# Up projection of an encoder block: first operands and weight sums issued ahead of the last token tile's norm, partial results kept in the u tile

## The chip, the cores and the metric

One program on one core of a Trainium2 chip. The metric is the device time of one execution in microseconds (us); the time of the kernel before is the median of three runs. Engines are TensorE (PE in the profile, PEld for its weight loads), VectorE (DVE), ScalarE (ACT), GpSimd (POOL) and SyncE (SP), which here issues the DMAs.

## The reference, cut to what matters

One layer of an encoder block on 1024 tokens of width 1024: a token mixer, a cross-attention into 256 memory tokens, and a gated MLP. Each has an RMSNorm before and after. What the change touches is the passage from the cross-attention's output to the MLP:

```python
y = memory_cross_attention(h, mem_n, w_mem_q[l], w_mem_kv[l], w_mem_o[l])
x = x + rmsnorm(y, norm_mem_post[l])
h = rmsnorm(x, norm_ffn_pre[l])
y = conv_gated_ffn(h, w_up[l], ffn_dw[l], ffn_dw_b[l], w_down[l])
...
def conv_gated_ffn(h, w_up, ffn_dw, ffn_dw_b, w_down):
    u = jnp.einsum("bsd,df->bsf", h, w_up)                # 1024 -> 2 x 2816
    u = dwconv_centred(u, ffn_dw, ffn_dw_b)               # width 3, along the tokens
    gate, val = u[..., :D_FF], u[..., D_FF:]
    return jnp.einsum("bsf,fd->bsd", jax.nn.gelu(gate, approximate=True) * val, w_down)
```

## The kernel before, in words

**Number format.** Every f32 operand of a matmul is split into a high part (a ScalarE cast) and a low part (source minus high part, on VectorE or GpSimd). A product is then three matmuls: high by high, high by low, low by high (`gemm3_multi`, lines 94 to 101).

**Cross-attention output (lines 701 to 712).** For each of eight token tiles (128 tokens), `cross_gemm` multiplies by the eight weight tiles `Uw`. `cross_norm` does the rest: a square with a sum on ScalarE (line 609), the reciprocal root on GpSimd (lines 85 and 86), scaling and residual on VectorE (lines 611 and 612), a store of x2, then a second square (709), a second root and the scaling to `h3` (711).

**Operands of the up projection's token side (lines 714 to 736).** `cross_operands` transposes h3 on TensorE, copies it to the raw tiles `b11`, `b21` (tokens 0 to 511) or `b12`, `b22` (the others), and from token tile 4 on forms the differences t1 to t4 (line 697), each in the place of a tile that it no longer needs. `b_split` (lines 688 to 694) makes high and low parts. Differences are on VectorE except t3, which is on GpSimd.

**Up projection (lines 752 to 827).** The product of the weights and tokens, each as 2 by 2 blocks, is done with seven block products in place of eight. There are 22 feature indices `fi`; each takes a gate tile `rg` and a value tile `rv` of the weights. `up_first(fi)` splits rg into `a1` and makes products p1 and p2, which need b11 and b21 alone, so tokens 0 to 511. `up_operands(fi)` forms the weight sums s12 and s34 on GpSimd from rg and rv (lines 775 to 778) and splits them into `a2`, `a3` and `a22`. `up_finish(fi)` does the other five products with t1, t2, b22, t3 and t4, adds up the quarters of `u`, runs the convolution, GELU and the product of gate and value, and stores the result. A half-finished sum stands in a tile `q`. After token tile 7's norm the kernel issues `up_first` for fi 0 and 1, then `cross_operands(7)`; from then on `up_first(fi)`, `up_operands(fi)`, `up_finish(fi - 1)`.

**What sets the order.** The program is written with a tile framework. It places each engine's instructions at compile time by a timeline of its own; the order on each engine is then fixed and the engine runs its queue in order. Tiles of one tag share a fixed number of buffers, and a later tile of a tag takes its buffer behind the earlier ones. Tag "w" has seven buffers (Uw, then a1, u, a2, a3, a22), tag "tmp" four (x2, h3, q, s12, s34), "raw" three (x1r, wg, wv), "a" fifteen (the operands' high and low parts among them), PSUM tag "B" four (pTs, p1 to p7).

Of the kernel before, what the change touches and what calls it, by code (L numbers as in the profile page):

```python
# [33 lines left out]
def encoder_block(ctx: ExitStack, tc: tile.TileContext, x, xT, mem, w_a, w_q, w_kv, w_mkv, w_mqT,  # L34
                  w_mo, w_out, w_up, w_down, cols, rows, g10, rope, out):
    nc = tc.nc
# [16 lines left out]
    def tmp(name):  # L53
        return tmpp.tile([128, 1024], F32, tag="tmp", name=name)
# [55 lines left out]
    def W(shape, name):  # L110
        return wp.tile([128] + shape, F32R, tag="w", name=name)
# [503 lines left out]
    def load_raw(src, name):  # L615
        r = raw(name)
        nc.sync.dma_start(out=r, in_=src)
        return r
# [21 lines left out]
    for t in range(8):  # L640
        h, tt = t // 4, t % 4
        y = psS("y1")
        tok_gemm(y, mxh[h], mxl[h], wo, tt)
        xr = gE[:, 1, :]
# [3 lines left out]
        j = tmp("junk2")  # L648
# [40 lines left out]
    def b_split(name, ts_):  # L689
        if name not in BO:  # L690
            BO[name] = (A([4, 512], f"{name}h"), A([4, 512], f"{name}l"))
        src, (hi, lo) = BR[name], BO[name]
        nc.scalar.copy(out=hi[:, :, ts_], in_=src[:, :, ts_])
        nc.vector.tensor_tensor(out=lo[:, :, ts_], in0=src[:, :, ts_], in1=f(hi[:, :, ts_]), op=ALU.subtract)

    def b_sub(dst, in0, in1, ts_, eng):
        eng.tensor_tensor(out=BR[dst][:, :, ts_], in0=BR[in0][:, :, ts_], in1=BR[in1][:, :, ts_], op=ALU.subtract)
# [14 lines left out]
        return j  # L712

    def cross_operands(t, j):
        h, tt = t // 4, t % 4
        ts_ = slice(tt * 128, tt * 128 + 128)
        if t == 4:
            BR["b12"], BR["b22"] = A([4, 512], "r_b12", F32), A([4, 512], "r_b22", F32)
            BR["t1"], BR["t2"], BR["t3"], BR["t4"] = BR["b11"], BR["b22"], BR["b12"], BR["b21"]
        for g in range(2):  # L720
            p = psB("pTs")
            for k in range(4):
                tr(p[:, k * 128:k * 128 + 128], j[:, (4 * g + k) * 128:(4 * g + k + 1) * 128])
            nc.scalar.copy(out=BR[f"b{g + 1}{h + 1}"][:, :, ts_], in_=p.rearrange("p (k t) -> p k t", k=4))
        if h == 0:
            b_split("b11", ts_)
            b_split("b21", ts_)
        else:
            b_sub("t1", "b12", "b11", ts_, nc.vector)
            b_split("t1", ts_)  # L730
            b_split("b22", ts_)
            b_sub("t3", "b22", "b12", ts_, nc.gpsimd)
            b_sub("t2", "b22", "t1", ts_, nc.vector)
            b_split("t2", ts_)
            b_split("t3", ts_)
            b_sub("t4", "t2", "b21", ts_, nc.vector)
            b_split("t4", ts_)
# [3 lines left out]
    def a_split(dst, src, eng):  # L741
        nc.scalar.copy(out=dst[:, 0, :], in_=src)  # L742
        eng.tensor_tensor(out=dst[:, 1, :], in0=src, in1=f(dst[:, 0, :]), op=ALU.subtract)  # L743
# [8 lines left out]
    H0, H1 = slice(0, 512), slice(512, 1024)  # L752
    ups, firsts, rgs = {}, {}, {}

    def up_first(fi):

        rg = rgs.pop(fi) if fi in rgs else load_raw(w_up[fi, 0], "wg")
        a1 = W([2, 2, 512], "a1")
        a_split(a1[:, 0], rg[:, H0], nc.gpsimd)
        a_split(a1[:, 1], rg[:, H1], nc.gpsimd)  # L760
        u = wp.tile([128, 2, 1024], F32, tag="w", name="u")
        q = tmp("q")
        p1, p2 = psB("p1"), psB("p2")
        product(p1, a1[:, 0], "b11")
        nc.scalar.copy(out=q[:, H0], in_=p1)
        product(p2, a1[:, 1], "b21")
        nc.vector.tensor_tensor(out=u[:, 0, H0], in0=p2, in1=q[:, H0], op=ALU.add)
        firsts[fi] = (rg, u, q)

    def up_operands(fi):  # L770

        rg, u, q = firsts.pop(fi)
        rv = load_raw(w_up[fi, 1], "wv")
        s12, s34 = tmp("s12"), tmp("s34")
        nc.gpsimd.tensor_tensor(out=s12[:, H0], in0=rv[:, H0], in1=rv[:, H1], op=ALU.add)
        nc.gpsimd.tensor_tensor(out=s12[:, H1], in0=s12[:, H0], in1=rg[:, H0], op=ALU.subtract)
        nc.gpsimd.tensor_tensor(out=s34[:, H0], in0=rg[:, H0], in1=rv[:, H0], op=ALU.subtract)
        nc.gpsimd.tensor_tensor(out=s34[:, H1], in0=rg[:, H1], in1=s12[:, H1], op=ALU.subtract)
        a2, a3 = W([2, 2, 512], "a2"), W([2, 2, 512], "a3")
        a_split(a2[:, 0], s12[:, H1], nc.vector)  # L780
        a_split(a2[:, 1], s12[:, H0], nc.vector)
        a_split(a3[:, 0], s34[:, H1], nc.vector)
        a_split(a3[:, 1], s34[:, H0], nc.vector)
        if fi % 2 == 0:
            a22[0] = W([2, 2, 512], "a22")
        a_split(a22[0][:, fi % 2], rv[:, H1], nc.gpsimd)
        ups[fi] = (a2, a3, a22[0][:, fi % 2], u, q)
# [41 lines left out]
    UP_PRE = 2  # L829
    for t in range(8):  # L830
        if t == 6:
            for fi in range(UP_PRE):
                rgs[fi] = load_raw(w_up[fi, 0], "wg")
        j = cross_norm(t, *cross_gemm(t))
        if t == 7:
            for fi in range(UP_PRE):
                up_first(fi)
        cross_operands(t, j)
# [248 lines left out]
```

## Time and profile before

| | |
|---|---|
| median of three runs | 1479.98 us (1477.62 to 1480.1) |
| profiled execution | 1478.46 us; span from first to last instruction 1476.7 us |
| busy share of the span | PE 94%, PEld 79%, DVE 74%, POOL 48%, ACT 47% |
| mean granted TensorE clock | 0.983 of full speed |

The span is 1.8 us less than the profiled execution's time. Busy shares are averages over stages with different limits: the token tiles' norms and operands of the passage between two matmul stages take 758 to 800 us of the span, the up projection runs on to about 1205 us, the down projection to the end.

### The profile page before, as it was taken

Reading aid. Unit: us, or ns where it says so; the run is one execution under the profiler, and the core shown is the slowest. Engines: PE = TensorE matmul, PEld = TensorE weight load, DVE = VectorE, ACT = ScalarE, POOL = GpSimd, SP = SyncE. Lnnn points to the kernel's source line nnn. Section 1 sums busy time; section 2 is a strip of 40 time slices with the busy share of each in tenths; the row PEclk is TensorE's granted clock in tenths of the full one; section 3 lists DMA queues with packets and bytes.
Section 4 is the critical chain, followed back from the end, with each engine's and each line's share of the span. In section 5 each row is a group of like instructions: output and inputs, shape, how many; then the busy total and the mean of one; then the engine's idle time right before and its main releaser. Section 6 shows DMA issues by size and latency. Waiting matters only on the chain.

```text
span 1476.7 us, 18881 instructions
## 1 busy us (share of the span) xinstructions
PE 1392.0 (94%) x7020; PEld 1165.0 (79%) x7020; DVE 1099.4 (74%) x1323; ACT 700.5 (47%) x1192; POOL 707.2 (48%) x627
## 2 busy tenths in 40 slices
PE   7999999889999999999997999999999997978895
PEld 5889988678988888888875888888888875756784
DVE  7499898899999534335468777777777789996676
ACT  6325653688888424334435444444444443323442
POOL 6628787711111414002137555444445449697456
PEclk9999999999999999999998999999999999999998
DMA  6316770000000524013223222222222292334145
GB/s 208 128 48 207 260 237 15 20 1 1 1 2 29 178 94 141 31 43 129 93 79 114 87 86 86 86 87 86 86 87 79 95 375 100 106 130 143 42 130 192
DMA packets 49515, 152.77 MB, mean 103 GB/s; under 512 B 9104, under 2 KB 9360, under 8 KB 49424
## 3 DMA queue, kind: packets, MB, share of 16 engines
q1 hardware_dynamic: 49424, 151.58, 30.8%
q8 instruction: 55, 0.90, 0.3%
q14 instruction: 36, 0.29, 0.1%
HBM read 119.05 MB, written 32.51 MB: 103 GB/s over the span
## 4 chain that ended last, share of the span: by engine, by line
PE 65%; DVE 15%; POOL 6%; issue 5%; DMA 5%; ACT 3%; SPq 0%; POOLq 0%; DVEq 0%; ACTq 0%
PE p L97 9%; PE p L98 9%; PE p L100 9%; DVE op L891 4%; PE y L98 4%; PE y L100 4%; PE y L97 4%; PE pPT L81 3%; PE sc L100 2%; PE sc L97 2%; PE sc L98 2%; DVE acts L891 2%; PE po L555 2%; PE sp L524 2%; PE sp L525 2%
## 5 line engine op out<-in xcount | busy, mean ns | idle before, releaser
L91 PE MATMUL yd<-op 128*128 128x512 f32 x308 | 126.8, 413 | 31.9 <-DVE op L891 16.0
L295 DVE SCALAR_TENSOR_TENSOR cacc<-conv,col,cacc 128x1009 f32<-128x1009 f32 (+14 forms) x120 | 145.8, 1273 | 4.7 <-ACT cacc L242 4.5
L92 PE MATMUL yd<-op 128*128 128x512 f32 x308 | 123.4, 404 | 1.8 <-DVE op L891 1.7
L923 ACT CAST op<-acts 128x512 fp32r<-128x512 f32 x77 | 47.6, 621 | 129.9 <-PE yd L92 47.6
L891 DVE TENSOR_TENSOR op<-acts,op 128x512 fp32r<-128x512 f32 x77 | 88.7, 1158 | 26.0 <-ACT op L923 25.8
L742 ACT CAST a<-s 128x512 fp32r<-128x512 f32 x88 | 50.6, 620 | 113.4 <-PE p L100 55.4
L91 PEld LDWEIGHTS yd<-op 128*128 128x128 f32 x308 | 60.2, 196 | 55.1 <-POOL op L891 23.5
L90 PE MATMUL yd<-op 128*128 128x512 f32 x308 | 98.4, 394 | 0.0
L743 POOL TENSOR_TENSOR a<-wg,a 128x512 fp32r<-128x512 f32 x44 | 62.5, 1441 | 72.9 <-ACT a L742 72.9
L793 DVE SCALAR_TENSOR_TENSOR c<-u,col,c 128x1023 f32<-128x1023 f32 x44 | 56.7, 1288 | 49.4 <-ACT c L792 49.3
L743 DVE TENSOR_TENSOR a<-s,a 128x512 fp32r<-128x512 f32 x88 | 72.3, 835 | 27.8 <-ACT a L742 27.5
L545 DVE TENSOR_TENSOR PL<-pPT,PH 128x512 fp32r<-128x512 f32 x128 | 82.7, 680 | 5.0 <-ACT PH L544 4.6
L85 POOL TENSOR_SCALAR rt<-ss 128x1 f32<-128x1 f32 (+1 forms) x43 | 13.0, 302 | 150.4 <-ACT x L609 75.8
L527 DVE TENSOR_REDUCE nm<-sp 128x1 f32<-128x1024 f32 x64 | 78.0, 1219 | 2.9 <-PE sp L525 1.8
L530 ACT ACTIVATE P<-sp,nm 128x1024 f32<-128x1024 f32 x64 | 72.2, 1128 | 8.9 <-PE pPT L81 5.1
L792 ACT ACTIVATE c<-u,col 128x1024 f32<-128x1024 f32 x44 | 53.2, 1210 | 48.7 <-DVE u L803 46.8
L544 ACT CAST PH<-pPT 128x512 fp32r<-128x512 f32 x128 | 69.3, 593 | 13.5 <-PE pPT L81 12.7
L92 PEld LDWEIGHTS yd<-op 128*128 128x128 f32 x308 | 60.1, 195 | 16.2 <-DVE op L891 4.2
L81 PE MATMUL pPT<-ident,P 128*128 128x128 f32 x512 | 68.6, 274 | 3.7 <-DVE PL L545 2.3
L90 PEld LDWEIGHTS yd<-op 128*128 128x128 f32 x308 | 58.8, 191 | 12.6
L81 PEld LDWEIGHTS pPT<-ident,P 128*128 128x128 f32 x512 | 58.6, 140 | 12.3 <-DVE PL L545 3.9
L743 POOL TENSOR_TENSOR a<-wv,a 128x512 fp32r<-128x512 f32 x22 | 31.9, 1468 | 74.6 <-ACT a L742 60.5
(352 smaller groups left out, 4553.7 us busy)
## 6 DMA issues: line engine op xcount, KB each, us to landing
st<-in_w_down_dram SPq DMA_DIRECT2D x43, 512.0 KB, 3.8
wg<-in_w_up_dram SPq DMA_DIRECT2D x22, 512.0 KB, 4.1
wv<-in_w_up_dram SPq DMA_DIRECT2D x22, 512.0 KB, 3.9
act_d<-u SPq DMA_DIRECT2D x22, 512.0 KB, 2.9
acts<-act_d SPq DMA_DIRECT2D x22, 512.0 KB, 9.1
wmkv_r<-in_w_mkv_dram SPq DMA_DIRECT2D x16, 512.0 KB, 4.0
x_d<-x SPq DMA_DIRECT2D x16, 512.0 KB, 2.9
wmq_r<-in_w_mqT_dram SPq DMA_DIRECT2D x8, 512.0 KB, 3.5
```

What stands on the lines that cost most here:

```text
L81: nc.tensor.transpose(out=out_, in_=in_, identity=ident)
L90: nc.tensor.matmul(out=ps, lhsT=sh, rhs=mh, start=first, stop=False)
L91: nc.tensor.matmul(out=ps, lhsT=sh, rhs=ml, start=False, stop=False)
L92: nc.tensor.matmul(out=ps, lhsT=sl, rhs=mh, start=False, stop=last)
L97: nc.tensor.matmul(out=p, lhsT=sh, rhs=mh, start=first, stop=False)
L98: nc.tensor.matmul(out=p, lhsT=sh, rhs=ml, start=False, stop=False)
L100: ins = nc.tensor.matmul(out=p, lhsT=sl, rhs=mh, start=False, stop=last)
L295: nc.vector.scalar_tensor_tensor(out=acc[:, t0:t1_], in0=a[:, t0 + o:t1_ + o], scalar=cc(C_DW + c * 31 + j), in1=acc[:, t0:t1_], op0=ALU.m ...
L527: nc.vector.reduce_max(out=nm, in_=sp, axis=AX.X, negate=True)
L545: nc.vector.tensor_tensor(out=PL[dst], in0=p3, in1=f(PH[dst]), op=ALU.subtract)
L743: eng.tensor_tensor(out=dst[:, 1, :], in0=src, in1=f(dst[:, 0, :]), op=ALU.subtract)
L891: eng.tensor_tensor(out=dst, in0=in0, in1=in1, op=op)
```

## The change

1. `up_first`'s split of the weights becomes `up_first_operands(fi, engs)`, where the two low parts can go to different engines. For fi 0 and 1 it is called after token tile 7's matmuls and before its norm, with one low part on GpSimd and one on VectorE; in the other iterations it stays where it was, with both on GpSimd.
2. The load of rv and the four weight sums become `up_sums(fi)`, called for fi 0 right after token tile 7's norm, before `up_first` of 0 and 1.
3. `q` is no longer a tile of tag "tmp" but the second half of `u`.
4. In `cross_operands` of tokens 512 and up, b22 is split before t1, and token tile 7's t3 is formed on VectorE.

```diff
     def cross_operands(t, j):
+        third = nc.gpsimd if t < 7 else nc.vector
...
             b_sub("t1", "b12", "b11", ts_, nc.vector)
+            b_split("b22", ts_)
             b_split("t1", ts_)
-            b_split("b22", ts_)
-            b_sub("t3", "b22", "b12", ts_, nc.gpsimd)
+            b_sub("t3", "b22", "b12", ts_, third)
...
-    def up_first(fi):
-
+    a1s = {}
+
+    def up_first_operands(fi, engs):
         rg = rgs.pop(fi) if fi in rgs else load_raw(w_up[fi, 0], "wg")
         a1 = W([2, 2, 512], "a1")
-        a_split(a1[:, 0], rg[:, H0], nc.gpsimd)
-        a_split(a1[:, 1], rg[:, H1], nc.gpsimd)
+        a_split(a1[:, 0], rg[:, H0], engs[0])
+        a_split(a1[:, 1], rg[:, H1], engs[1])
+        a1s[fi] = rg, a1
+
+    def up_first(fi):
+
+        if fi not in a1s:
+            up_first_operands(fi, (nc.gpsimd, nc.gpsimd))
+        rg, a1 = a1s.pop(fi)
         u = wp.tile([128, 2, 1024], F32, tag="w", name="u")
-        q = tmp("q")
+        q = u[:, 1, :]
...
-    def up_operands(fi):
-
-        rg, u, q = firsts.pop(fi)
+    sums = {}
+
+    def up_sums(fi):
+        rg = a1s[fi][0] if fi in a1s else firsts[fi][0]
         rv = load_raw(w_up[fi, 1], "wv")
         s12, s34 = tmp("s12"), tmp("s34")
...
+        sums[fi] = rv, s12, s34
+
+    def up_operands(fi):
+
+        if fi not in sums:
+            up_sums(fi)
+        rv, s12, s34 = sums.pop(fi)
+        rg, u, q = firsts.pop(fi)
...
-        j = cross_norm(t, *cross_gemm(t))
+        y, xr = cross_gemm(t)
         if t == 7:
+            for fi in range(UP_PRE):
+                up_first_operands(fi, (nc.gpsimd, nc.vector))
+        j = cross_norm(t, y, xr)
+        if t == 7:
+            up_sums(0)
             for fi in range(UP_PRE):
                 up_first(fi)
```

## Rows read from the trace of the kernel before

**Rows 1.** Busy time by stretch: engines' busy us (instructions), granted clock, DMA share.
```profile
core 0: us, PE busy (x) PEld busy (x) DVE busy (x) ACT busy (x) POOL busy (x), PEclk, DMA share, GB/s
...
800.00:1190.00 390.00, 389.90 (x1719) 322.19 (x1718) 281.40 (x330) 165.53 (x228) 193.44 (x146) 1.00 0.29 96
...
757.80:795.20 37.40, 25.32 (x110) 19.79 (x108) 34.51 (x36) 20.45 (x39) 22.43 (x18) 0.92 0.21 71
...
795.00:800.00 5.00, 4.77 (x13) 3.64 (x13) 4.99 (x9) 2.75 (x6) 3.49 (x1) 0.58 0.00 0
```

**Rows 2.** Timeline of TensorE: start us, us, what, count, [idle before, releaser].
```profile
768.55 1.06 PE L81 MATMUL pTs<-ident,h 128*128 128x128 f32 x8 [1.06 <-DVE h L711]
...
779.17 0.80 PE L97 MATMUL p<-b11h,a 128*128 128x512 f32 x1 [4.08 <-ACT a L742]
...
781.04 1.55 PE L81 MATMUL pTs<-ident,h 128*128 128x128 f32 x8
...
790.03 0.50 PE L97 MATMUL p<-t1h,a 128*128 128x512 f32 x1 [2.88 <-ACT a L742]
...
795.23 0.79 PE L98 MATMUL p<-t2l,a 128*128 128x512 f32 x1 [4.09 <-DVE t2l L694]
```

**Rows 3.** Timeline of ScalarE between token tile 7's norm and its operands.
```profile
769.57 1.02 ACT L609 ACTIVATE x<-y 128x1024 f32<-128x1024 f32 x1
...
778.50 1.14 ACT L742 CAST a<-wg 128x512 fp32r<-128x512 f32 x2
...
784.92 0.59 ACT L765 COPY q<-p 128x512 f32<-128x512 f32 x1 [0.53 <-PE p L100]
```

**Rows 4.** Timeline of GpSimd in the same stretch.
```profile
772.67 1.30 POOL L697 TENSOR_TENSOR r_b<-r_b,r_b 128x512 f32<-128x512 f32 x1
...
779.19 3.63 POOL L743 TENSOR_TENSOR a<-wg,a 128x512 fp32r<-128x512 f32 x2 [0.68 <-ACT a L742]
...
784.84 1.74 POOL L775 TENSOR_TENSOR s<-wv 128x512 f32<-128x512 f32 x1
```

**Rows 5.** Timeline of the DMA queue, and of the page the wv loads' time to landing.
```profile
776.81 15.17 SPq L617 DMA_DIRECT2D wv<-in_w_up_dram  x2
...
wv<-in_w_up_dram SPq DMA_DIRECT2D x22, 512.0 KB, 3.9
```

**Rows 6.** Timeline of VectorE from token tile 6's residual to token tile 7's t2.
```profile
760.28 2.31 DVE L612 TENSOR_TENSOR x<-x,x1r 128x1024 f32<-128x1024 f32 x1
...
762.51 1.79 DVE L694 TENSOR_TENSOR t1l<-r_b,t1h 128x512 fp32r<-128x512 f32 x1
...
764.38 2.23 DVE L694 TENSOR_TENSOR b22l<-r_b,b22h 128x512 fp32r<-128x512 f32 x2
...
772.74 1.28 DVE L611 SCALAR_TENSOR_TENSOR x<-y,rs,gG 128x1024 f32<-128x1024 f32 x1 [0.72 <-POOL rs L86]
...
775.14 1.22 DVE L612 TENSOR_TENSOR x<-x,x1r 128x1024 f32<-128x1024 f32 x1
...
778.72 1.27 DVE L711 SCALAR_TENSOR_TENSOR h<-x,rs,gG 128x1024 f32<-128x1024 f32 x1
779.91 1.77 DVE L694 TENSOR_TENSOR t2l<-r_b,t2h 128x512 fp32r<-128x512 f32 x1
782.75 0.69 DVE L697 TENSOR_TENSOR r_b<-r_b,r_b 128x512 f32<-128x512 f32 x1 [1.07 <-ACT r_b L724]
783.90 1.53 DVE L694 TENSOR_TENSOR b22l<-r_b,b22h 128x512 fp32r<-128x512 f32 x1 [0.46 <-ACT b22h L693]
785.36 1.78 DVE L694 TENSOR_TENSOR t1l<-r_b,t1h 128x512 fp32r<-128x512 f32 x1
787.06 1.75 DVE L697 TENSOR_TENSOR r_b<-r_b,r_b 128x512 f32<-128x512 f32 x1
788.84 3.94 DVE L694 TENSOR_TENSOR t3l<-r_b,t3h 128x512 fp32r<-128x512 f32 x3
792.70 0.68 DVE L767 TENSOR_TENSOR u<-p,q 128x512 f32<-128x512 f32 x1
...
794.50 0.68 DVE L694 TENSOR_TENSOR t2l<-r_b,t2h 128x512 fp32r<-128x512 f32 x1
```

## The prediction, made before the change was run

> **What bounds the kernel now.** I read the forty slices of the page first: TensorE is 90% busy or more in most of the cross-attention and of the up projection, with a dip where one passes into the other. The stretch view then says where the change can count. From 800 to 1190 us TensorE is busy 389.9 of 390 us at full clock, so nothing done for the other engines inside the up projection's steady iterations can show [rows 1]. In the passage before it the picture turns: from 757.8 to 795.2 us TensorE is busy 25.3 of 37.4 us and VectorE 34.5 [rows 1]. So the change is worth what it does to those 37 us.
>
> The timeline of TensorE names four waits there: 1.06 us for token tile 6's h3, 4.08 us for the second tile pair's split weights, 2.88 us for the first weight sum's cast, and 4.09 us for the low part of t2 [rows 2]. Together they are 12.1 us. After the long ones the clock is low: in the stretch from 795 to 800 us it is 0.58 of full speed, so 5 x 0.42 = 2.1 us more are lost, and the eight transposes at 781 us take 1.55 us where they took 1.06 [rows 1, 2]. About 15 us, 12.1 + 2.1 + 0.5 and a little for the few matmuls at 779 us, is the most that could be won.
>
> The next view is what ended the waits, by engine. The 4.08 us wait ends with ScalarE's cast of a1 at 778.50 [rows 3]. The weights had been loaded long before; what was late is the buffer: tile u stands ahead of the second a1 in tag "w" and its first writer is VectorE's add of p2. In the same way GpSimd's first weight sum starts at 784.84, though the wv load issued at 776.81 lands 3.9 us later, at 780.7 [rows 4, 5]; s12 stands behind the second q in tag "tmp", and that q is first written at 784.92 [rows 3]. The last wait ends at the bottom of VectorE's queue. After the copies of token tile 7 it runs t1, three low parts, t2's difference, three leftover low parts of t3 (3.94 us), u's add, two more, and only at 794.50 the t2 low part that TensorE waits for [rows 6].
>
> VectorE is slow there for a reason that the rows show: the same 128x512 subtraction takes 0.69 us at 782.75 and 1.53 to 1.79 us in the rows at 762.51, 779.91, 783.90, 785.36 and 787.06, and each of these lies beside a GpSimd elementwise operation (the pair from 779.19 and the sum at 784.84 are two of the stretches) [rows 4, 6]. I count nine such operations: those five, one of the pair at 764.38, two of the three at 788.84, and the residual add at 760.28 (2.31 us against 1.22 at 775.14). Their excess is 1.09 + 1.11 + 0.95 + 1.09 + 0.85 + 1.10 + 1.07 + 2.06 = 9.3 us, 1.04 us per GpSimd operation.
>
> **The change part by part.** The sum is made against the profiled execution, 1478.46 us, which is 1.5 us below the median of the runs.
>
> *Splits of the first two tile pairs ahead of the norm.* The 4.08 us wait goes, since the second a1 no longer stands behind u. But TensorE only reaches the next wait sooner: the 24 matmuls of p1 and p2 for fi 1 then run from 775.1 to about 780.5, and everything after needs token tile 7. What this brings to the end is the transposes. h3 of tile 7 is ready at 778.72 + 1.27 = 779.99; they ended at 781.04 + 1.55 = 782.59, 2.60 us later; for tile 6, where nothing stood in the way, they began at the end of the 1.06 us wait and took 1.06 [rows 2, 6]. With the wait gone and the clock full I expect about 1.2 us from h3 to their end: **-1.4 us**. Ends: 0, if they are queued behind all of fi 1's products and these start late; -1.4.
>
> *VectorE's and GpSimd's load.* VectorE gets three more operations (two low parts, t3 of tile 7), and GpSimd loses these three. One uncollided VectorE operation costs 0.60 us from start to start (792.70 to 794.50 is three steps, 1.80 us) [rows 6]: +1.8 us. Of the three GpSimd operations taken away two had stretched a VectorE operation (the second low part of the first a1, t3 beside 783.90) and the second a1's other low part fell into a pause. So two excesses of 1.04 go, -2.1 us. Sum **-0.3 us**. Ends: -3.1 if two more of the weight sums fall into VectorE's pauses and -0.3 + 3.1 = +2.8 if each of the three moved operations is itself stretched.
>
> *The order b22 before t1 and ScalarE's queue.* Token tile 7's square began at 769.57, 2.1 us after its matmuls ended (768.55 - 1.06 = 767.49), behind casts of t2 that themselves waited for VectorE [rows 2, 3]; VectorE then stood 0.72 us for the norm's root [rows 6]. With b22's low part early, t2's differences can run before 767 us, and I expect this 0.72 us back: **-0.7 us**. Ends: +0.7, if t1's low part is now what is late, and -2.1, the whole delay.
>
> *Weight sums ahead.* With q out of tag "tmp" the sums start when wv lands, up to 784.84 - 780.7 = 4.1 us sooner [rows 4, 5]. The 2.88 us wait that a2's cast ended then goes, yet t2's low part would still end the pause. What is won is that product p5, which needs t1 and the first sum alone, can run in the pause: 12 matmuls. In the steady stage 390 us hold 1719 of them, 0.227 us each [rows 1], so 2.7 us leave the path after the wait; the two low parts it needs go ahead of t2's on VectorE, 2 x 0.60 = 1.2 us. Net **-1.5 us**. Ends: 0 if the planner keeps p5 behind t2 as now, -2.7 if the two low parts fall into pauses.
>
> *q in u.* No instruction is added; the adds read and write the same sizes. u is taken about a product's time (2.7 us) sooner in each iteration. In the steady stage TensorE hides it [rows 1]; if it made the second product wait for a buffer, each of 20 iterations could cost up to that 2.7 us. The end above zero I leave out of the range's middle, since ScalarE and GpSimd are busy less than half of that stage. **0.**
>
> Sum: -1.4 - 0.3 - 0.7 - 1.5 = -3.9 us, **1474.6 us**. The steady stage and the down projection should shift as a whole.
>
> **A rule against it.** The rows of VectorE show the stretching; they also show one operation that isn't stretched, the scaling at 772.74, which reads PSUM and takes 1.28 us beside GpSimd's 772.67 [rows 4, 6]. The Trainium skill, "GPSIMD Engine Reference", section "Key points", says that GpSimd shares its SBUF interfaces with VectorE, so that VectorE instructions with two SBUF inputs contend. By that rule a low part moved to VectorE, with two SBUF inputs, pays beside its sister half on GpSimd; the trace agrees for every pair that it shows, 1.53 to 1.79 us against 0.69.
>
> **Rivals.**
>
> *The order on VectorE changes too.* If the new plan puts t2's low part ahead of the leftover low parts of t3 (3.94 us) and of u's add and the two behind it (1.8 us), the pause shrinks by up to 5.7 us more: 1474.6 - 5.7 = 1468.9. For it: none of these is needed before t2's. Against: three of them come from earlier token tiles and nothing in the change moves them. Chance 0.20.
>
> *The idle time only moves.* VectorE is busy 92% of the passage and its work stays the same within 0.3 us. If p5 stays behind t2 and the square stays late, only part of the transposes' term is left: about 1.2 us, 1477.3. For it: three of TensorE's four waits end, directly or one step back, in VectorE's queue. Chance 0.25.
>
> *The plan hardly changes.* The casts stay where they are because their buffers are still late: 1478.5, within 0.5. Against: the two tiles that blocked are the ones moved. Chance 0.07.
>
> *The moved low parts collide.* The two low parts of a1 are placed in VectorE's queue before token tile 6's h3 and token tile 7's scaling, where it is already busy without a break from 758 to 772 us; with t3 they pay 1.70 us each instead of 0.60 (785.36 to 787.06 is such a step) [rows 6], 5.1 us on the path, against 1.4 from the transposes and nothing else won: +3.7, 1482.2 us. It decides as soon as both stand ahead of tile 7's scaling and more than two of the three are stretched. This is what the rule on shared interfaces would make of the change. Chance 0.13.
>
> **How the numbers follow.** The forecast has the rest, 0.35, with a range of its own from 1472 to 1477. A measurement of this kernel can tell about 0.2%, 3 us, from no change. Faster by more than that takes most of the forecast (0.29), the changed order (0.20) and a little of the moved idle time (0.06): 0.55. Slower by more is the collision and a sliver for the u buffer: 0.14. Within 0.2% is the rest, 0.31. The range for 8 in 10 runs from 1467.5 (changed order, with 1.4 us for the sums in pauses) to 1480.5, which takes in both cases of no change with the 1.5 us between profiled execution and median, and about half the way to the collision.
>
> **What would show it.** Right: no wait for a1's cast near 779 us; transposes of tile 7 within 0.5 us of h3; GpSimd's sums starting within 1 us of wv's landing; matmuls of p5 before the wait for t2's low part; VectorE still over 90% busy in the passage. Wrong: h3 of tile 6 or 7 later than 768.4 and 780.0 us, TensorE waiting in the steady stage, or a down projection that doesn't simply shift.

## The result, and the profile after: slower by 0.5 to 0.7%

The changed kernel took 1490.3 us (median; 1487.3 to 1490.9) against 1479.9 us before: ratio 1.007, 95% interval 1.0054 to 1.0086. A second series (e1 below) gave 1488.0 us and 1.0053 (1.0036 to 1.0069). The forecast, 1474.6 us with a range up to 1480.5, was wrong in sign. One of the five executions, the profiled one, was disturbed (1585.6 us) and is left out of the range, and the profile shown here is that of e1, with a span of 1488.1 us.

All times below are places in that one execution. Where two kernels are compared, the place is counted from the end of the last cross-attention matmul (767.50 us before, 766.90 us after), since the profiles of this study reach it between 763.6 and 769.3 us without any pattern.

| us after the last cross-attention matmul | before | after (e1) |
|---|---|---|
| h3 of token tile 6 done | 0.9 | 3.3 |
| h3 of token tile 7 done | 12.5 | 14.6 |
| t2's last low part done | 27.7 | 28.6 |
| t4's last low part done | 31.9 | 39.5 |
| first of the adds behind the second products | 35.4 | 44.4 |
| first pair's products done | 42.9 | 50.7 |
| second pair's products done | 62.3 | 69.9 |
| last up matmul | 437.9 | 445.2 |

So the loss is all there by the end of the first pair, 7.8 us later than before, and it arises between two rows: t2's low part is 0.9 us behind, t4's 7.6 us. From the first pair's end to the last up matmul both kernels take the same, 395.1 us before and 394.5 after. From the last cross-attention matmul to the end of the span the two differ by 12.0 us (709.2 and 721.2). Of the rest 1.6 us come in the first two down products (e7), and 3 us in the later ones, which take 194.3 to 197.5 us in the profiles of this study without a pattern. The medians differ by 8.7 us alone (e1's series), so these 3 us need not be the change's.

Stretches of the kernel after (columns as in [rows 1]); the first and the last line stand beside those of [rows 1]:

```profile
757.80:795.20 37.40, 29.82 (x122) 24.03 (x121) 33.51 (x42) 20.63 (x38) 22.93 (x15) 0.86 0.21 71
795.20:812.00 16.80, 7.25 (x32) 5.64 (x31) 13.72 (x10) 5.50 (x10) 16.30 (x11) 0.86 0.51 157
...
788.10:793.40 5.30, 4.71 (x10) 3.42 (x11) 5.30 (x10) 3.71 (x7) 2.63 (x1) 0.50 0.26 87
...
802.40:812.10 9.70, 0.05 (x1) 0.00 (x0) 9.67 (x8) 2.80 (x5) 9.20 (x7) 0.76 0.62 206
...
820.00:1190.00 370.00, 370.00 (x1634) 306.45 (x1634) 265.85 (x311) 156.27 (x215) 176.13 (x133) 1.00 0.28 91
```

Up to 795.2 us TensorE is ahead: 122 matmuls where [rows 1] has 110. Then it does 32 where the kernel before, in the line below, does 64. From 802.4 to 812.1 us it stands, while VectorE and GpSimd, both busy for over 9 of the 9.7 us, complete 8 and 7 instructions. The same stretch before:

```profile
795.20:812.00 16.80, 16.72 (x64) 13.13 (x65) 12.86 (x18) 7.29 (x12) 14.23 (x8) 0.88 0.48 153
```

TensorE's timeline after (columns as in [rows 2]):

```profile
770.37 1.94 PE L81 MATMUL pTs<-ident,h 128*128 128x128 f32 x8 [3.46 <-DVE h L711]
...
778.10 0.39 PE L97 MATMUL p<-b11h,a 128*128 128x512 f32 x1
...
783.55 1.04 PE L81 MATMUL pTs<-ident,h 128*128 128x128 f32 x8
788.13 0.79 PE L97 MATMUL p<-t1h,a 128*128 128x512 f32 x1 [3.55 <-ACT t1h L693]
789.49 0.79 PE L98 MATMUL p<-t1l,a 128*128 128x512 f32 x1 [0.56 <-DVE t1l L694]
...
791.36 0.63 PE L100 MATMUL p<-t1h,a 128*128 128x512 f32 x1
791.79 0.63 PE L97 MATMUL p<-t1h,a 128*128 128x512 f32 x1
...
812.15 0.77 PE L97 MATMUL p<-t4h,a 128*128 128x512 f32 x1 [9.70 <-DVE u L821]
```

In place of the four waits of [rows 2] (1.06, 4.08, 2.88 and 4.09 us) there are 3.46, 3.55, 0.56 and 9.70: 17.3 us of idle time instead of 12.1. The longest is released by VectorE's adds of products to u, whose PSUM banks the p4 matmuls need. And behind each of these waits the matmuls start 0.43 us apart (791.36 to 791.79), not 0.23: the clock is granted at 0.50 there, 1.2 of 2.4 GHz. Between the last cross-attention matmul and the first pair's end 108 product matmuls run in both kernels; those more than 0.3 us apart number 15 before, with 3.1 us in excess of 0.227 each, and 24 after, with 5.1 us. Idle time +5.2 and clock +2.0 make 7.2 of the 7.8 us.

VectorE after (as in [rows 6]), from token tile 6's norm to the adds:

```profile
765.34 1.28 DVE L744 TENSOR_TENSOR a<-wg,a 128x512 fp32r<-128x512 f32 x2
...
768.95 1.27 DVE L711 SCALAR_TENSOR_TENSOR h<-x,rs,gG 128x1024 f32<-128x1024 f32 x1
...
773.25 1.28 DVE L611 SCALAR_TENSOR_TENSOR x<-y,rs,gG 128x1024 f32<-128x1024 f32 x1 [0.45 <-POOL rs L86]
...
780.18 1.28 DVE L711 SCALAR_TENSOR_TENSOR h<-x,rs,gG 128x1024 f32<-128x1024 f32 x1
...
791.75 2.49 DVE L694 TENSOR_TENSOR t3l<-r_b,t3h 128x512 fp32r<-128x512 f32 x4
...
794.76 0.69 DVE L694 TENSOR_TENSOR t2l<-r_b,t2h 128x512 fp32r<-128x512 f32 x1
798.53 1.11 DVE L744 TENSOR_TENSOR a<-s,a 128x512 fp32r<-128x512 f32 x1 [3.08 <-ACT a L743]
799.57 6.83 DVE L694 TENSOR_TENSOR t4l<-r_b,t4h 128x512 fp32r<-128x512 f32 x4
806.33 5.08 DVE L744 TENSOR_TENSOR a<-s,a 128x512 fp32r<-128x512 f32 x3
811.33 3.45 DVE L821 TENSOR_TENSOR u<-p,u 128x512 f32<-128x512 f32 x5
```

GpSimd beside it (as in [rows 4]):

```profile
781.43 1.30 POOL L785 TENSOR_TENSOR s<-wv 128x512 f32<-128x512 f32 x1 [2.41 <-DMA wv<-in_w_up_dram]
...
790.77 5.83 POOL L744 TENSOR_TENSOR a<-wv,a 128x512 fp32r<-128x512 f32 x1 [3.88 <-ACT a L743]
796.56 1.28 POOL L785 TENSOR_TENSOR s<-wv 128x512 f32<-128x512 f32 x1
...
799.05 1.75 POOL L744 TENSOR_TENSOR a<-wv,a 128x512 fp32r<-128x512 f32 x1
800.76 1.74 POOL L786 TENSOR_TENSOR s<-s,wg 128x512 f32<-128x512 f32 x1
...
809.15 1.70 POOL L786 TENSOR_TENSOR s<-s,wg 128x512 f32<-128x512 f32 x1
```

Here is where t4's low parts go. VectorE's next low part belongs to the second pair (a<-s at 798.53) and waits 3.08 us for a sum that GpSimd, held up by a 5.83 us operation, brings at 797.84. From 799.57 to 811.33 VectorE runs seven operations in 11.76 us, 1.68 us each, all beside GpSimd's sums and low parts; the last three are the second pair's as well, ahead of the adds that TensorE waits for. The kernel before, in the same place, VectorE first and then GpSimd:

```profile
794.50 0.68 DVE L694 TENSOR_TENSOR t2l<-r_b,t2h 128x512 fp32r<-128x512 f32 x1
795.10 1.88 DVE L743 TENSOR_TENSOR a<-s,a 128x512 fp32r<-128x512 f32 x3
796.91 2.48 DVE L694 TENSOR_TENSOR t4l<-r_b,t4h 128x512 fp32r<-128x512 f32 x4
...
801.83 1.11 DVE L743 TENSOR_TENSOR a<-s,a 128x512 fp32r<-128x512 f32 x1 [1.84 <-ACT a L742]
802.86 1.40 DVE L803 TENSOR_TENSOR q<-p,q 128x512 f32<-128x512 f32 x2
```

```profile
796.51 4.63 POOL L775 TENSOR_TENSOR s<-wv 128x512 f32<-128x512 f32 x1 [4.89 <-DVE a L743]
801.10 2.99 POOL L743 TENSOR_TENSOR a<-wv,a 128x512 fp32r<-128x512 f32 x2
```

There GpSimd's queue stood until 796.51, because the second pair's s12 waited for one of the first pair's to come free, and its next operations were queued behind that: the low parts a<-wv come at 801.10, where after the change the first starts at 790.77, and one sum is done by 801.10 where after there are three by 802.5. VectorE ran seven operations of the same kind in 4.2 us (795.10 to 799.31), 0.60 each, and met one low part of the second pair ahead of the adds. The one sum that lay beside them, from 796.51, didn't stretch them; it took 4.63 us itself (see the last section). With q out of the tag "tmp" that wait has gone, and GpSimd has eight operations beside VectorE's seven where it had one.

From t2's last low part to the first add VectorE needs 15.9 us where it needed 7.7. Of the 8.2 us more, 7.6 are the seven operations at 1.68 us instead of 0.60; the rest is the longer wait for a sum (3.08 us against 1.84), less one operation.

### The profile page after: what moved, and what is told of

Same layout as the page of the kernel before. It is cut to its first block, busy times and chain, and to the rows that moved or that the text cites. A ratio compares the mean times of both kernels' runs of the same rounds, so it can differ in the third digit from the quotient of the medians.

```text
span 1583.8 us, 18876 instructions
## 1 busy us (share of the span) xinstructions
PE 1518.3 (96%) x7020; PEld 1208.4 (76%) x7020; DVE 1101.9 (70%) x1326; ACT 702.6 (44%) x1192; POOL 706.9 (45%) x624
## 4 chain that ended last, share of the span: by engine, by line
PE 82%; DVE 9%; DMA 3%; issue 2%; ACT 2%; POOL 2%; SPq 0%; POOLq 0%; DVEq 0%; ACTq 0%
PE p L97 9%; PE p L100 9%; PE p L98 9%; PE y L98 4%; PE y L97 4%; PE y L100 4%; PE pPT L81 3%; DVE op L914 3%; PE sp L524 2%; PE sc L98 2%; PE yd L91 2%; PE sc L100 2%; PE sc L97 2%; PE po L555 2%; PE yd L92 2%
## 5 line engine op out<-in xcount | busy, mean ns | idle before, releaser
L91 PE MATMUL yd<-op 128*128 128x512 f32 x308 | 130.7, 428 | 20.2 <-DVE op L914 11.4
L92 PE MATMUL yd<-op 128*128 128x512 f32 x308 | 128.8, 423 | 0.1
L914 DVE TENSOR_TENSOR op<-acts,op 128x512 fp32r<-128x512 f32 x77 | 93.3, 1220 | 26.9 <-ACT op L946 26.7
L821 DVE TENSOR_TENSOR u<-p,u 128x512 f32<-128x512 f32 x110 | 75.4, 686 | 44.7 <-PE p L100 44.2
L90 PE MATMUL yd<-op 128*128 128x512 f32 x308 | 105.9, 421 | 0.0
L81 PE MATMUL pPT<-ident,P 128*128 128x128 f32 x512 | 76.1, 297 | 1.6 <-DVE PL L545 1.0
L744 DVE TENSOR_TENSOR a<-s,a 128x512 fp32r<-128x512 f32 x88 | 63.6, 745 | 14.7 <-ACT a L743 14.7
```

What stands on the lines that cost most here:

```text
L81: nc.tensor.transpose(out=out_, in_=in_, identity=ident)
L90: nc.tensor.matmul(out=ps, lhsT=sh, rhs=mh, start=first, stop=False)
L91: nc.tensor.matmul(out=ps, lhsT=sh, rhs=ml, start=False, stop=False)
L92: nc.tensor.matmul(out=ps, lhsT=sl, rhs=mh, start=False, stop=last)
L914: eng.tensor_tensor(out=dst, in0=in0, in1=in1, op=op)
```

## Experiments

Theory A: the buffers freed by q let GpSimd form the sums of the second and third pair beside VectorE's chain; part of the loss is stretching (A1), part the order in which VectorE then meets its work (A2). Theory B: the a1 low parts moved to VectorE, ahead of tile 6's h3, are the loss. Theory C: q in u costs in the steady stage. The edits are made to the changed kernel unless it says otherwise. Ratios are against the kernel before on the same chip (its medians: 1479.3, 1479.0, 1479.8 and 1479.8 us in the four series).

| | us | ratio, 95% interval | first pair done | last up matmul to second down product | idle + clock in the passage |
|---|---|---|---|---|---|
| before | 1479 to 1480 | 1 | 42.9 | 76.9 | 12.1 + 3.1 |
| e1 changed kernel | 1488.0 | 1.0053 (1.0036, 1.0069) | 50.7 | 78.5 | 17.3 + 5.1 |
| e2 sums held | 1481.1 | 1.0012 (1.0002, 1.0023) | 40.3 | 79.1 | 8.6 + 4.6 |
| e3 held, GpSimd busy | 1491.0 | 1.0079 (1.0055, 1.0102) | 41.3 | 78.5 | |
| e4 before, with q in u | 1492.9 | 1.0089 (1.0069, 1.0109) | 54.0 | 78.2 | 19.3 + 6.7 |
| e5 first pair's adds first | 1486.5 | 1.0045 (1.0032, 1.0058) | 49.3 | 78.3 | |
| e6 q as before | 1482.4 | 1.0020 (1.0007, 1.0032) | 48.2 | 76.9 | 12.2 + 7.6 |
| e7 q in u from fi 4 on | 1485.6 | 1.0045 (1.0031, 1.0059) | 49.2 | 78.3 | |
| e8 q as before, sums held | 1480.6 | 1.0009 (0.9997, 1.0021) | 46.3 | 76.9 | 11.0 + 7.3 |
| e9 a1's low parts on GpSimd | 1489.1 | 1.0065 (1.0051, 1.0079) | 52.8 | 77.9 | |
| e10 e9 and e2 | 1482.2 | 1.0020 (1.0010, 1.0031) | 42.5 | 78.9 | |
| e11 e9, held, q in u for fi 0 to 3 | 1481.8 | 1.0017 (1.0007, 1.0026) | 42.6 | 76.9 | 11.5 + 3.0 |
| e12 e11, old order | 1480.7 | 1.0013 (1.0000, 1.0026) | 44.2 | 76.9 | |
| e13 held, q in u for fi 0 to 3 | 1479.1 | 0.9996 (0.9984, 1.0008) | 43.9 | 76.9 | 9.4 + 6.7 |
| e14 e13, old order | 1480.7 | 1.0007 (0.9996, 1.0017) | 46.2 | 76.9 | |
| e15 e13, low parts behind norm | 1481.2 | 1.0007 (0.9997, 1.0018) | 42.9 | 76.9 | |

("First pair done" counts from the last cross-attention matmul. "Idle + clock" is TensorE's idle time up to there, and what its product matmuls more than 0.3 us apart take in excess of 0.227 us each. One profile each; the times are medians of several runs, and a profiled execution lies up to 4.4 us from its median.)

**e1**, the changed kernel as it is:

> The changed kernel once more, for an undisturbed profile. Theory A (freed buffers: with q out of the tmp tag GpSimd forms the weight sums of fi 1 and 2 right behind those of fi 0, beside VectorE's chain t3, t4, t2, t4 low parts, and stretches nearly each of its operations from 0.6 to 1.7 us): about 1490 us, and between the end of the cross-attention's matmuls and the first u adds VectorE shows ten or more operations of about 1.75 us. Theory B (the moved operations: the two low parts of a1 and t3 of token tile 7 stand in VectorE's queue ahead of the norm and delay h3): about 1490 us, h3 of tile 7 more than 5 us later after the matmuls' end than the 12.5 us of the kernel before. Theory C (q in u: u is taken earlier and a buffer of tag w is short in the steady iterations): about 1490 us, TensorE idle time spread over the 22 iterations, 0.4 us in each.

It stands above. VectorE's stretched operations are eight, not ten; tile 7's h3 is 2.1 us later, not over 5; and TensorE has no idle time in the steady stage, which speaks against C.

**e2**, GpSimd's sums of the second and third pair wait for t4's last low part, by a one-column copy into the tile that they write:

```
         s12, s34 = tmp("s12"), tmp("s34")
+        if fi in (1, 2):
+            nc.gpsimd.tensor_copy(out=s12[:, 0:1], in_=f(BO["t4"][1][:, 3, 511:512]))
```

> The changed kernel, but the weight sums s12 of fi 1 and 2 first wait for the last low part of t4: a one-column GpSimd copy from it into s12, overwritten by the sum, is put ahead. Nothing else is changed. Theory A: the stretched operations go and the time falls to 1472 to 1480 us, at or below the kernel before. Theory B: the moved operations are still there, 1488 to 1492 us. Theory C: q is still in u, 1488 to 1492 us.

7 us come back, to 1.1 us above A's range, and the 9.7 us wait has gone. The first pair is done 10.4 us sooner than in e1, 2.6 us sooner than before the change. VectorE and GpSimd in the held kernel:

```profile
794.64 0.69 DVE L694 TENSOR_TENSOR t2l<-r_b,t2h 128x512 fp32r<-128x512 f32 x1
795.43 4.50 DVE L694 TENSOR_TENSOR t4l<-r_b,t4h 128x512 fp32r<-128x512 f32 x4
803.09 2.74 DVE L823 TENSOR_TENSOR u<-p,u 128x512 f32<-128x512 f32 x4 [3.15 <-PE p L100]
...
790.64 7.54 POOL L744 TENSOR_TENSOR a<-wv,a 128x512 fp32r<-128x512 f32 x2 [3.88 <-ACT a L743]
800.00 0.19 POOL L786 COPY s<-t4l 128x1 f32<-128x1 f32 x1 [1.82 <-DVE t4l L694]
```

So the sums that start sooner are the loss in the passage. Over the kernel before nothing is left of the 2.6 us: the second pair is done 21.1 us behind the first (19.4 before), and the first two down products take 2.2 us more. The copy changes both what lies beside VectorE's chain and VectorE's own order (the second pair's low parts now come behind t4's), and doesn't part A1 from A2.

**e3**, e2 with eight needless additions on GpSimd ahead of the copy, to have GpSimd beside VectorE without any work of VectorE depending on it:

```
+        if fi == 1:
+            for _ in range(8):
+                nc.gpsimd.tensor_tensor(out=s12[:, H0], in0=rv[:, H0], in1=rv[:, H1], op=ALU.add)
```

> As the held sums, but GpSimd does eight additions that nobody needs (the first sum of fi 1, over and over) while it would wait, so the sums stay late and VectorE's order stays that of the held kernel, only the company on GpSimd is back. Theory A in its port form (GpSimd's work beside VectorE's chain is the cost): back up to 1485 to 1491 us. A variant of A in which it is the order of VectorE's queue (low parts of fi 1 ahead of the first u adds) that costs: it stays at 1472 to 1481 us. Theories B and C: 1488 to 1492 us.

The loss came back, but not by the way that was to be tested. The first pair was done after 41.3 us, 1.1 us later than in e2; but the additions held up the second pair's own sums, and TensorE stood there (waits of TensorE: us in total, times, longest us):

```profile
PE p L97 <- ACT a L743: 10.4, 1, 10.4
```

So its time says nothing between A1 and A2. Its first pair does say something. Beside the additions t4's low parts are stretched as in e1:

```profile
798.05 6.70 DVE L694 TENSOR_TENSOR t4l<-r_b,t4h 128x512 fp32r<-128x512 f32 x4
805.69 3.47 DVE L826 TENSOR_TENSOR u<-p,u 128x512 f32<-128x512 f32 x5 [0.94 <-PE p L100]
```

Yet the adds behind them still wait for TensorE, and the first pair is done sooner than before the change (41.3 us against 42.9). So these four alone are not the loss: it takes more than them ahead of the adds.

**e4**, the kernel before with that one line of the change:

```
-        q = tmp("q")
+        q = u[:, 1, :]
```

> The kernel before with one edit: q is the second half of u instead of a tmp tile. Theory A: this alone frees the sums of fi 1 and 2 and brings most of the loss, 1485 to 1491 us. Theory B: no moved operation, 1476 to 1481 us. Theory C: 1488 to 1492 us with idle time in the steady iterations.

It alone costs 13.6 us, more than the whole change (and 1.9 us more than A's range had); what else the change does gives some 5 us back. The steady stage takes 394.4 us, so it isn't C. GpSimd's sums of the second pair start at 794.32 and VectorE's chain is stretched over its whole length:

```profile
794.01 5.73 DVE L694 TENSOR_TENSOR t3l<-r_b,t3h 128x512 fp32r<-128x512 f32 x4
799.66 1.77 DVE L697 TENSOR_TENSOR r_b<-r_b,r_b 128x512 f32<-128x512 f32 x1
...
794.32 1.53 POOL L775 TENSOR_TENSOR s<-wv 128x512 f32<-128x512 f32 x1 [0.89 <-issue]
```

No moved low part of a1 is in this kernel: the loss needs no B.

**e5**, GpSimd's queue as in e1, VectorE's low parts of the second pair put behind the first pair's fifth add:

```
+        if fi == 1:
+            with tc.issue_after(adds[0].ins):
+                up_operands(1)
```

> The changed kernel with VectorE's queue alone altered: the four low parts of fi 1 stand behind the fifth add of fi 0 instead of ahead of its first; GpSimd's queue is that of the changed kernel, so the sums of fi 1 and 2 are as early as there. Theory A1 (the stretching alone costs): the t4 low parts are as long as in the changed kernel and the up projection ends as late, about 1486 to 1490 us. Theory A2 (early sums make the planner put the low parts of fi 1 ahead of the adds that free PSUM; 3.1 us of waiting for GpSimd and eight stretched operations of 1.7 us then stand before the first add): TensorE's 9.7 us wait for u's add goes, the first pair is finished near 807 us as with the held sums instead of 817.6, the up projection ends near 1205 instead of 1212, and the time is 1478 to 1483 us.

The time is in A1's range, 1.5 us below e1's with overlapping intervals, and the first pair is done 1.4 us sooner. That is not what the order (A2) is worth, for something else differs in the two profiles. VectorE has 12 additions or subtractions of over 1.4 us between tile 7's h3 and the first pair's end, where e1 has 8 and e2 has 3. t3's four low parts, which e1 runs in 2.49 us behind the same instructions, are among them:

```profile
791.17 6.81 DVE L694 TENSOR_TENSOR t3l<-r_b,t3h 128x512 fp32r<-128x512 f32 x4
```

So a stretched chain brings the loss without the second pair's low parts ahead of the adds. In e1 these stand there too, three of them stretched and one behind a wait of 3.08 us. By e1's rows the stretching is the larger part (7.6 of 8.2 us), but no run took the order away and left the stretching as it was: what A2 is worth in e1 stays open.

**e6**, q in its own tile again, the rest of the change kept:

```
-        q = u[:, 1, :]
+        q = tmp("q")
```

> The changed kernel with q back in a tmp tile, all else as changed. Theory A: the sums of fi 1 wait for the low parts of fi 0, those of fi 2 much longer; the loss shrinks to 1476 to 1484 us. But in VectorE's queue one low part of fi 1 now stands ahead of t2's low part; if GpSimd is late with that sum, TensorE waits there, and it is 1484 to 1490 us. Theory B (the moved operations): 1488 to 1492 us.

5.6 us come back, and 3.5 us remain over the kernel before. In the passage TensorE is idle as long as before, 12.2 us, but 36 matmuls run at the lower clock (7.6 us of excess against 3.1): the waits are cut otherwise, and the clock is low behind most of them.

**e7**, q in u only where the steady stage runs:

```
-        q = u[:, 1, :]
+        q = tmp("q") if fi < 4 else u[:, 1, :]
```

> The changed kernel with q a tmp tile for the first four fi and the second half of u from then on: the passage as without q in u, the end of the up projection as with it. If the 4.7 us that the changed kernel loses behind the up projection's last matmul come from q in u there (other placing of the down projection's operands), this is 4 to 5 us slower than the kernel with q in tmp throughout; if they come from the passage, the two agree within 1.5 us.

The up projection's steady stage takes 395.5 us (395.1 before): C falls. Yet this kernel is 3 us slower than e6, between the two expectations. 1.4 us of it are seen in the first two down products, 78.3 us against 76.9 in all eight kernels with q in "tmp" at the end and 77.9 to 79.1 in the seven others with it in u. TensorE's waits in these two products in e1, and in e13 (below), where q is in u for the first four pairs only:

```profile
PE yd L91 <- DVE op L914: 9.3, 2, 7.3
```

```profile
PE yd L91 <- DVE op L917: 6.7, 3, 3.4
```

The first of them stands 7.3 us in one piece; that the last u, taken a product sooner for q, holds back the buffer of a first operand is what I suppose, and no run took it apart further.

**e8**, e6 with a hold for the second pair's sums, on t4's first low part:

```
+        if fi == 1:
+            nc.gpsimd.tensor_copy(out=s12[:, 0:1], in_=f(BO["t4"][1][:, 0, 127:128]))
```

> The changed kernel with q back in a tmp tile and the first sum of fi 1 held until the first low part of t4 (a one-column GpSimd copy, overwritten). Theory A2: no sum of fi 1 beside the t3 and t2 chain and no low part of fi 1 ahead of t2's or t4's; about 3 us ahead of the kernel before at the end of the first pair, and with the down projection as before 1474 to 1479 us. Theory B: 1484 us or more.

The kernel before again, within the interval. A2's expectation isn't met either: the first pair is done 3.4 us later than before, not 3 us sooner. None of the gains of the other edits shows.

**e9**, a1's moved low parts back on GpSimd, still ahead of the norm:

```
-                up_first_operands(fi, (nc.gpsimd, nc.vector))
+                up_first_operands(fi, (nc.gpsimd, nc.gpsimd))
```

> The changed kernel, with the two moved low parts of a1 given to GpSimd instead of VectorE; all else stays, q in u too. Theory A (the loss is GpSimd's sums of the later pairs running beside VectorE's chain behind token tile 7's norm): h3 of tiles 6 and 7 comes about 2 us sooner after the last cross-attention matmul (0.9 and 12.5 us, as before the change, where the changed kernel has 3.3 and 14.6), but the wait of TensorE for u's add stays over 5 us, and the time stays at 1485 to 1488 us. Theory B (the moved low parts ahead of tile 6's h3 are the loss): the wait for u's add is under 3 us and the time is 1478 to 1481 us.

The wait for u's adds stays (9.4 us) and so does the loss, as A has it. But h3 of tile 6 is later still, 4.9 us and not 0.9: I had overlooked that the norm's rt and rs run on GpSimd. Its queue:

```profile
757.60 7.34 POOL L744 TENSOR_TENSOR a<-wg,a 128x512 fp32r<-128x512 f32 x4
765.03 0.52 POOL L85 TENSOR_SCALAR rt<-ss 128x1 f32<-128x1 f32 x1
765.63 0.88 POOL L86 TENSOR_TENSOR rs<-rt,mhalf 128x1 f32<-128x1 f32 x1
```

rt starts 1.4 us after the last cross-attention matmul (763.62 here) where e1 has it 1.95 us before it. The first pair's end is 2.0 us later than in e1, as much as tile 7's h3 (2.1): here a late h3 is passed on whole. From e2 to e10 it is passed on in part, 2.2 of 3.5 us.

**e10**, e9 with the hold of e2:

> The held kernel (GpSimd's sums of the second and third pair wait for the last low part of t4) with the two moved low parts of a1 on GpSimd as well. Theory A with B as a small part: h3 of tiles 6 and 7 about 2 us sooner after the last cross-attention matmul, the first pair's products done 38 to 39 us after it (40.3 in the held kernel), and 1479 to 1480 us, since q in u still costs some 1.4 us in the first two down products. Rival (the last low part of t4, not h3, sets the end, and two more GpSimd operations stretch VectorE instead): the first pair's products still 40 us or more after it, 1481 us or more.

The hold gives its 7 us again, and the low parts on GpSimd cost 2.2 us at the first pair's end against e2; at 42.5 and 1482.2 us the rival is right, not the first expectation.

**e11**, e9, with q in u for the first four pairs only and the holds on t4's low part of token tile 4 (second pair) and of tile 7 (third pair):

```
-        q = u[:, 1, :]
+        q = u[:, 1, :] if fi < 4 else tmp("q")
...
+        if fi in (1, 2):
+            last = 127 if fi == 1 else 511
+            nc.gpsimd.tensor_copy(out=s12[:, 0:1], in_=f(BO["t4"][1][:, 3, last:last + 1]))
```

> What the earlier runs point to, together: the moved low parts of a1 on GpSimd; q in u for the first four pairs only, so that no q stands in u when the down projection begins; the second pair's sums held until t4's low part of token tile 4 and the third pair's until that of tile 7. If the parts add, the first pair's products end 39 to 41 us after the last cross-attention matmul, the first two down products take 76.9 us as before, and the time is 1476 to 1478 us. If the gains in the passage are given back at the second pair, as in the held kernel, it is 1479 to 1481 us and TensorE waits over 3 us for casts of a.

The down products are at 76.9 us, as expected. The first pair is done at 42.6 us, later than expected, the second 20.9 us behind it (19.4 before), and the time, 1481.8 us, is above both ranges and nearer the second.

**e12**, e11 with b22 split behind t1 again:

```
-            b_split("b22", ts_)
             b_split("t1", ts_)
+            b_split("b22", ts_)
```

> The same as the one before it, with b22 split behind t1 again as in the kernel before. If the order of b22 and t1 is worth the 0.7 us forecast, this is some 0.7 us slower than that one; if the order only moves ScalarE's casts, the two agree within 0.5 us; if it lets h3 of token tile 7 and t3's low parts go first, this one is 1 to 2 us faster.

1 us faster than e11, with overlapping intervals: the order is worth nothing that can be seen, and isn't the 0.7 us gain that was forecast.

**e13**, e11 with a1's moved low parts on VectorE as in the change:

> The changed kernel with the moved low parts of a1 on VectorE as they are; q in u for the first four pairs only; the second pair's sums held until t4's low part of token tile 4, the third pair's until that of tile 7. If what the held kernel gave back came from q in u at the down projection (1.4 us) and from the second pair's late sums (some 2 us), and GpSimd's moved low parts cost the passage 2 us in the kernel of e11: first pair done 40 to 41 us after the last cross-attention matmul (42.6 in e11), the first two down products 76.9 us, 1477 to 1479.5 us. If the passage's gain is given back at the second pair whatever is done, 1480 to 1482 us, with the second pair done 21 us behind the first instead of 19.4.

1479.1 us, ratio 0.9996: the whole loss of the change is gone with its two causes, the early sums of the later pairs and q in u at the start of the down projection. The second pair is 19.3 us behind the first, as the first expectation has it, but the first pair is done at 43.9 and not at 40 to 41. Beyond undoing the loss nothing is won, and the passage shows why: TensorE's idle time is 9.4 us where it was 12.1, and the matmuls at the lower clock cost 6.7 us where it was 3.1. From 788 to 795 us, right behind a wait of 3.27 us:

```profile
788.00:795.00 7.00, 6.40 (x16) 5.00 (x17) 7.00 (x9) 2.92 (x6) 3.29 (x2) 0.52 0.37 125
```

**e14**, e13 with the old order of b22 and t1:

> The same as e13 with b22 split behind t1 again. By the forecast's step for this order it is 0.7 us slower than e13; by the pair e11 and e12 (1481.8 and 1480.7 us, second pair 20.9 and 19.0 us behind the first) it is about 1 us faster, with tile 7's h3 some 1.5 us earlier and t2's low part some 1.5 us later.

1.7 us slower than e13, where e12 was 1 us faster than e11, each with overlapping intervals: no step that holds.

**e15**, all low parts of a1 on GpSimd, the second pair's written behind tile 7's norm:

```
-            for fi in range(UP_PRE):
-                up_first_operands(fi, (nc.gpsimd, nc.vector))
+            up_first_operands(0, (nc.gpsimd, nc.gpsimd))
         j = cross_norm(t, y, xr)
         if t == 7:
+            up_first_operands(1, (nc.gpsimd, nc.gpsimd))
             up_sums(0)
```

> The same as e13 with all four low parts of a1 on GpSimd, and the second pair's two placed behind token tile 7's norm instead of ahead of it, though still ahead of the first u. If the low parts ahead of tile 6's h3 are what makes it late: h3 of tile 6 at 0.9 us after the last cross-attention matmul (3.3 in the changed kernel, 4.9 in e9 to e12), and TensorE's wait for its transposes at 1.1 us. The 4.08 us wait near 779 us comes back in part if the low parts now lie in GpSimd's queue behind the first sums. Time 1477 to 1480 us; 1482 us or more if the wait comes back whole.

Neither of the two came about: the plan put all four low parts on GpSimd ahead of rt just as in e9 (one group of four from 758.47 us), and h3 of tile 6 again comes at 4.9 us. The time, 1481.2 us, lies between the two ranges. How the passage would go with a1 off both norms wasn't tried in another way. No version beats the kernel before.

## Why the prediction was wrong

**The step that failed is "q in u: 0".** It looked for what the change could cost in the tag that q enters, found u's time hidden in the steady stage, and was right there: that stage takes the same within 0.6 us. It didn't ask the same of the tag that q leaves. The step before it used the answer ("With q out of tag "tmp" the sums start when wv lands"), but for the first pair alone. The same release takes 4.89 us of waiting out of GpSimd's queue in front of the second pair's sums, and everything behind them moves up beside VectorE, at the one place where VectorE sets the pace. e4 (that line alone, +13.6 us) and e2 (the sums held, -7 us) show it. With the loss undone (e13) the kernel is as fast as before, so the -3.9 us of the other terms didn't show either.

**VectorE's and GpSimd's load: -0.3, ends -3.1 and +2.8.** The count went by operations that the change adds or removes between 757.8 and 795.2 us. The collisions that matter are of operations that are neither added nor removed, only free to start sooner, and they lie behind 795 us: seven of VectorE's at 1.68 us instead of 0.60, 7.6 us. The price of 1.04 us per collision was right for one; their number was not. (The lower end was also added up wrongly: two excesses below -0.3 are -2.4, not -3.1.) I had a rival of colliding operations, at +3.7 us, with the wrong ones in it: a1's moved low parts run at 0.60 us in e1 (two in 1.28 us from 765.34), unstretched.

**Transposes: -1.4.** The 4.08 us wait went, as forecast. But the transposes of tile 7 start at 783.55, right behind the 24 matmuls of the second pair that begin at 778.10: the end that was called "queued behind all of fi 1's products", worth 0. They are done 17.7 us after the last cross-attention matmul, 15.1 before [rows 2]. The rest is tile 6's h3: at 770.22 where 768.4 was named as the sign of a wrong step. It stands behind the two low parts of a1 and four more operations on VectorE, and TensorE's first wait grew from 1.06 to 3.46 us. Theory B is true to that extent: tile 7's h3 is 2.1 us later, of which 0.9 us are left at t2's last low part. It is not what made the kernel slower.

**The order of b22 and ScalarE's queue: -0.7.** The square of tile 7 began earlier (767.78, 0.9 us after its matmuls, against 2.1), but the wait for the norm's root is still 0.45 us, since GpSimd's rt took 3.1 us there. e11 to e14 show no effect of the order with one sign.

**Weight sums ahead: -1.5.** Half right. The first sum starts at 781.43, where wv lands; the cast's wait of 2.88 us has gone; p5's 12 matmuls run ahead of t2's low part. They run at 0.43 us each: 5.1 us, not 2.7, since a wait of 3.55 us for t1 stands right before them. Forecast and kernel agree about what is moved; what was missed is that the matmuls moved into this pause run at half the clock (0.50 from 788.10 to 793.40). Part of the held kernels' gain goes the same way (e2: idle -3.5, clock +1.5; e13: -2.7 and +3.6).

**The first two down products.** The forecast had the down projection "simply shift". With q in u at its beginning they take 78.5 us, not 76.9.

**What the rule had to say.** The rows show VectorE's and GpSimd's SBUF operations at 1.68 and 1.70 us beside each other, and VectorE's five adds that read PSUM at 0.69 us beside GpSimd's (811.33 in e1). The Trainium skill, "GPSIMD Engine Reference", section "Key points", says that the two share SBUF interfaces; the trace agrees. It had been weighed for the moved operations only. And the prediction read too much into the rows with its "for every pair that it shows": in the kernel before, t4's four low parts (from 796.91) have two SBUF inputs and run at 0.60 us beside GpSimd's sum; there it is the sum that takes longer, 4.63 us.

## What to carry to other kernels

A tile taken out of a rotating pool is an edit in two places: ask of the tag that it leaves which instructions were waiting there, on which engine, and what runs beside them once they no longer wait. A wait that looks like waste can be what keeps two engines apart. And count a matmul that is moved into a pause at the clock that the rows show behind the pause, not at that of the steady stage.

## What the runs showed of the hardware that was not expected

VectorE and GpSimd share their time in two ways. In one both run in step, 1.68 to 1.75 us per operation. In the other VectorE runs at full speed and GpSimd's one operation lasts until VectorE pauses: 5.83 us in e1, 4.63 us before. Both of these end 1.15 us after VectorE's pause begins (at 795.45 and 799.99), where one such operation alone takes 1.28 us (796.56 in e1). Both ways occur at the same place with the same instructions: t3's low parts run one way in e1 and the other in e5 (above). Another such pair is e2, from 790.43:

```profile
790.43 1.29 DVE L744 TENSOR_TENSOR a<-s,a 128x512 fp32r<-128x512 f32 x2
791.63 2.49 DVE L694 TENSOR_TENSOR t3l<-r_b,t3h 128x512 fp32r<-128x512 f32 x4
```

with e13, from 789.66:

```profile
789.66 2.38 DVE L744 TENSOR_TENSOR a<-s,a 128x512 fp32r<-128x512 f32 x2
791.96 3.57 DVE L694 TENSOR_TENSOR t3l<-r_b,t3h 128x512 fp32r<-128x512 f32 x4
...
789.88 3.29 POOL L744 TENSOR_TENSOR a<-wv,a 128x512 fp32r<-128x512 f32 x2 [3.89 <-ACT a L743]
```

In e2 GpSimd's two low parts take 7.54 us (shown above) and VectorE's six operations 3.6; in e13 they take 3.29, and VectorE's six 5.8. GpSimd's first starts 0.21 and 0.22 us after VectorE's in the two. What decides between the ways stays open; that it may be behind the spread of several kernels here (1481.0 to 1488.5 us in e5) is a supposition.
